# HGRN values projected token-major in the front and loaded by the heads, four gates turned into fillers

## The chip, the cores and the metric

The kernel runs on one NeuronCore of a Trainium2 chip. The metric is the time of one execution on the device in microseconds (us), the median of several runs. The engines named are PE (TensorE matmul; PEld its weight load), DVE (VectorE), ACT (ScalarE), POOL (GpSimd) and SP (SyncE, which issues most DMAs).

## The reference, cut to what matters

One layer of a hybrid mixer: 512 latent tokens `x` and 256 context tokens `ctx`, model width 1024. Both are normalised and modulated, and multiplied by one wide matrix `w_in`. Its columns feed branch A (four heads of gated DeltaNet), branch B (four heads of HGRN2) and 24 groups of 128 gate columns, which only the latent tokens need. For branch B each head has 128 columns for q, for the values `i_b` and for the two forget gates:

```python
(qkv, a_f, a_b, be_f, be_b, g_a, q_b, i_b, f_f, f_b, g_b, m_a, m_b) = split_last(h @ w_in, IN_SIZES)
q_b = to_heads(jax.nn.silu(q_b), H_B).astype(f32)
v_b = to_heads(i_b, H_B).astype(f32)
...
# HGRN2, per chunk: S_t = diag(f_t) S_{t-1} + k_t v_t^T with k_t = 1 - f_t
s_next = f_end_c[..., None] * s + jnp.einsum('bhck,bhcv->bhkv', k_end_c, v_c)
att = jnp.einsum('bhik,bhjk,bhijk->bhij', q_c, k_c, pair)
o = jnp.einsum('bhck,bhkv->bhcv', q_c * jnp.exp(lg_c), s) + jnp.einsum('bhij,bhjv->bhiv', att, v_c)
...
return (jax.nn.sigmoid(m_a) * ya + jax.nn.sigmoid(m_b) * yb) @ w_out
```

The context is scanned in both directions for the state alone, then the latent tokens. The values of all 768 tokens are used; the outputs of the mixers are normalised, gated, projected up, merged, multiplied by `w_out` and added to `x`; a SwiGLU with its own modulation follows.

## The kernel before, in words

Every large product is done in float32 precision as three matmuls of reduced-precision parts (high x high, high x low, low x high). `split` loads a piece of weight to `raw`, ACT casts it to `hi` (L100), DVE subtracts for `lo` (L102), and `mm3` issues the three matmuls for each of the eight slices of 128 model columns (L110). The normalised tokens stand as `hhi`, `hlo` (latent, 512) and `chi`, `clo` (context, 256), with the model dimension on the partitions.

The front normalises the latent tokens slice by slice and feeds each slice at once to six accumulating products `pg0`, which are gates 16 to 21; their weights come as `wr` (128x768, one DMA for each slice, L239). Gates 22 and 23 (`rest[0:2]`) follow with code whose priority is lowered by 1500, with four quarters of the second modulation (`mwe`, `pmo`). A finished gate is copied by ACT to `gt` (L136) and stored to `gdram` (L137), from where it is loaded only after the mixers. `pab` is a small projection for branch A's decay.

The mixers are Python generators: `gdn_pair(0)` and `gdn_pair(2)` are streams G0 and G2 (two DeltaNet heads each), `hgrn(h)` is H0 to H3. The string `PLAN` says in which order steps of the streams are written: "H0:2" runs H0 for two yields, "F:2" writes two gates as fillers (`gate_low`), "N" and "aT" are modulation quarters. Behind X the branch A buffers are gone; the gates that are left and the rest of the modulation (`mwb`, issued on POOL's queue) are written with a priority lower by 5000, so they fill whatever H2's last steps leave open. A scheduler places each engine's instructions by priority and readiness, so an instruction may stand far from where its code is; each engine then executes in order.

An HGRN head has three projections (`h_z0`, `h_z1` for the forget gates over all tokens, `h_z2` for q), eight attention levels (`att`: level 7 and then `LEVELS` 0 to 6, four matmuls `h_pA` each, DVE operations `kq` L556, `AT` L536, `K` L558, `L` L559), then `values()`, then the two scans (`h_pk`, `h_pS`), the output `h_po` and its norm (`h__pt`, `h_y`). `values()` splits the head's 128 value columns, projects 512 latent and 256 context tokens with features on partitions (`h_zv`), copies them to `Z`, and transposes six blocks (`h_pv`) into `vh`, tokens on partitions. A DeltaNet pair builds `p_N`, inverts triangular blocks by 30 small DVE steps (`p_o1` to `p_o30` on `p_Z`), transposes the result (`p_T1`, `p_T2`, L745 and L746), scans, and ends with the transposes `p_pt` for its two heads.

After the mixers `branch` loads gates (`ug`) and mixer outputs (`uy`) from memory, `up` is the up-projection (`pup`), then `w_out` (`pwo`) and the SwiGLU (`pf`, `pfo`).

Of the kernel before, what the change touches and what calls it, by code (L numbers as in the profile page):

```python
# [7 lines left out]
F32 = mybir.dt.float32  # L8
# [5 lines left out]
P = 128  # L14
D = 1024
KT = 8
CTX = 256
SEQ = 512
TOK = 768
NH = 4  # L20
# [3 lines left out]
C_QKV, C_AB, C_GA, C_QB, C_IB, C_FF, C_FB, C_GB, C_MA, C_MB = (  # L24
    0, 1536, 1552, 2064, 2576, 3088, 3600, 4112, 4624, 5648)
# [3 lines left out]
MK = 4  # L29

PLAN = ("H0:1 G0:6 F:1 H1:3 G0:4 F:1 G2:3 G0:5 F:2 N:1 G0:1 H0:2 "
        "F:1 G0:99 H0:99 F:3 G2:4 H1:99 G2:4 F:1 G2:99 N:1 H3:99 aT:1 H2:1 X H2:99")


def shape_constants():
# [13 lines left out]
def body(tc, T, out, tap=None):  # L49
    nc = tc.nc  # L50
    PSUM = bass.MemoryType.PSUM
    W_IN = T["w_in"][0]
# [5 lines left out]
    with ExitStack() as root:  # L58
        def pool(name, bufs=1, side=None, **kw):
            return tc.tile_pool(name=name, bufs=bufs, side=side, reuse_waits="tile", **kw)  # L60
# [7 lines left out]
        dr = root.enter_context(tc.tile_pool(name="dr", bufs=1, space=bass.MemoryType.DRAM))  # L68
# [7 lines left out]
        def bank(tag, name):  # L76
            return ps_.tile([P, 512], F32, name=name, tag=tag, bufs=BANKS[tag])

        def pmm(name):
            return bank("mm", name)  # L80
# [3 lines left out]
        def split(srcs, kt, n, pool=None, dst=None):  # L84

            WN[0] += 1
            pool = pool or ring["w"]
            raw = pool.tile([P, kt, n], F32, name=f"raw{WN[0]}", tag="raw", bufs=2)
            c0 = 0
            for s in srcs:  # L90
                w = s.shape[1]
                nc.sync.dma_start(raw[:, :, c0:c0 + w], s.rearrange("(k p) f -> p k f", p=P))
                c0 += w
            if dst is not None:
                hi, lo = dst
                nc.scalar.copy(hi, raw[:, :, :])
                nc.vector.tensor_tensor(lo, raw[:, :, :], hi.bitcast(F32), op=ALU.subtract)
                return hi, lo
            hi = pool.tile([P, kt, n], F32R, name=f"hi{WN[0]}", tag="hi")
            nc.scalar.copy(hi[:, :, :], raw[:, :, :])  # L100
            lo = pool.tile([P, kt, n], F32R, name=f"lo{WN[0]}", tag="lo")
            nc.vector.tensor_tensor(lo[:, :, :], raw[:, :, :], hi.bitcast(F32), op=ALU.subtract)  # L102
            return hi, lo

        def mm3(ps, a, b, kt, start=True, stop=True):

            n, tot = 0, 3 * kt
            for k in range(kt):
                for u, v in ((0, 0), (0, 1), (1, 0)):
                    nc.tensor.matmul(ps, a[u](k), b[v](k), start=(start and n == 0), stop=(stop and n == tot - 1))  # L110
                    n += 1
# [6 lines left out]
        def feat(w, src, n, name, t0=0, tag="mm"):  # L118

            ps = bank(tag, name)  # L120
            mm3(ps[:, 0:n], [lambda k, t=t: t[:, k, :] for t in w], [lambda k, t=t: t[:, k, t0:t0 + n] for t in src], KT)
            return ps
# [5 lines left out]
        lat, ctx = (hhi, hlo), (chi, clo)  # L128
        gdram = dr.tile([24, P, SEQ], F32, name="gdram")
        ydram = dr.tile([8, P, SEQ], F32, name="ydram")  # L130
        gcols = [C_GA + P * i for i in range(4)] + [C_GB + P * i for i in range(4)]
        gcols += [C_MA + P * i for i in range(8)] + [C_MB + P * i for i in range(8)]

        def gate_out(i, ps, pool, tag="raw"):
            gt = pool.tile([P, SEQ], F32, name=f"gt{i}", tag=tag, bufs=3 if pool is ring.get("sp") else 2)
            nc.scalar.copy(gt[:, :], ps[:, :])  # L136
            nc.sync.dma_start(gdram[i, :, :], gt[:, :])  # L137
# [36 lines left out]


        NG0 = 6
        rest = [22, 23] + list(range(16))
        gs = early.enter_context(pool("gs"))
        s3_stack = ExitStack()
        s3 = s3_stack.enter_context(pool("s3"))  # L180
        with ExitStack() as st:
            s1 = st.enter_context(pool("s1"))
            sp = ring["sp"] = st.enter_context(pool("sp", 2))
# [15 lines left out]
            ident, UI, LI, US, LS = (sq[:, k * P:(k + 1) * P] for k in range(5))  # L199
# [35 lines left out]
            for d0, d1 in groups:  # L235
                load_mod(d0, d1)
                for e in range(d0, d1):
                    wr = wrs.pop() if wrs else s1.tile([P, NG0 * P], F32, name=f"wr{e}", tag="wr", bufs=5)
                    nc.sync.dma_start(wr[:, :], W_IN[P * e:P * e + P, C_MB:C_MB + NG0 * P])  # L239
                    wraws.append(wr)  # L240
                if d0 == 1:
                    r0 = 0
                    for key, pat_, cnt in small[1]:
                        kw = {"k": P} if key == "lb_logits" else {"p": P}
                        nc.sync.dma_start(rows[1][r0:r0 + cnt, :], T[key].rearrange(pat_, **kw) if pat_ else T[key])
                        r0 += cnt
# [95 lines left out]
            pg0 = [bank(t, f"pg0_{i}") for i, t in enumerate(("mm", "mm", "ga", "ga", "ga", "fa"))]  # L342
# [13 lines left out]
            for d in range(KT):  # L356
                if d in nxt:
                    modulation(*groups[nxt[d]])
                if d + 1 < KT:
                    prepare(d + 1)  # L360
                if d == 6:
                    norm_rows((0, 1))
                wh, wl = wparts[d]
                for n, (u, v) in enumerate(((wh, hhi), (wl, hhi), (wh, hlo))):
                    for i in range(NG0):
                        nc.tensor.matmul(pg0[i][:, :], u[:, P * i:P * i + P], v[:, d, :],
                                         start=(d == 0 and n == 0), stop=(d == KT - 1 and n == 2))
            for i in range(NG0):
                gate_out(16 + i, pg0[i], sp, "gt")
            for d in range(KT):  # L370
                normed(d, 1, (0, 1), chi, clo, "ha")
            dump("chi", chi.bitcast(F32))
# [26 lines left out]
            for i in rest[0:2]:  # L399
                w = [s1.tile([P, KT, P], F32R, name=f"rw{i}{j}") for j in range(2)]  # L400
                w = split([W_IN[:, gcols[i]:gcols[i] + P]], KT, P, dst=[t[:, :, :] for t in w])
                gate_out(i, feat(w, lat, SEQ, f"pgate{i}"), sp, "gt")
            for q in quarters[0:4]:
                mod_now(*q, s1.tile([P, KT, 256], F32, name="mwe%d%d" % q, tag="mw", bufs=6), nc.sync)
            del quarters[0:4]
# [3 lines left out]
        with s3_stack:  # L409
# [4 lines left out]
            for src, o, n in ((ctx, 0, CTX), (lat, CTX, SEQ)):  # L414
                ps = pmm(f"pab{o}")
# [23 lines left out]
            e = s3.tile([P, 6, 8], F32, name="e")  # L439
            nc.vector.scalar_tensor_tensor(e[:, :, :], zz[:, :, :], -1.0, zz[:, :, :], op0=ALU.mult, op1=ALU.max)  # L440
            nc.scalar.activation(e[:, :, :], e[:, :, :], AF.Exp, scale=-1.0)
            t = s3.tile([P, 6, 8], F32, name="t")
# [41 lines left out]
        def hgrn(h):  # L484

            n = f"h{h}_"
# [3 lines left out]
            q = hg.tile([P, SEQ], F32, name=n + "q", tag="q", bufs=2)  # L490
            vh = hg.tile([P, 6, P], F32, name=n + "v", tag="v")

            def values():
                w = split([W_IN[:, C_IB + P * h:C_IB + P * h + P]], KT, P)
                Z = hg.tile([P, TOK], F32, name=f"{n}Zv", tag="Z", bufs=2)
                for src, a, t in ((lat, CTX, SEQ), (ctx, 0, CTX)):
                    ps = feat(w, src, t, f"{n}zv_{a}")
                    nc.scalar.copy(Z[:, a:a + t], ps[:, 0:t])
                for g, cnt in ((0, 4), (4, 2)):
                    pv = pmm(f"{n}pv{g}")  # L500
                    for i in range(cnt):
                        nc.tensor.transpose(pv[:, P * i:P * i + P], Z[:, P * (g + i):P * (g + i + 1)], ident)
                    nc.scalar.copy(vh[:, g:g + cnt, :], pv[:, 0:P * cnt].rearrange("p (g k) -> p g k", k=P))

            for d in range(3):
                w = split([W_IN[:, (C_FB, C_FF, C_QB)[d] + P * h:(C_FB, C_FF, C_QB)[d] + P * h + P]], KT, P)
                m = TOK if d < 2 else SEQ
                Z = hg.tile([P, TOK], F32, name=f"{n}Z{d}", tag="Z", bufs=2)
                sg = hg.tile([P, TOK], F32, name=f"{n}sg{d}", tag="sg")
                for src, a, t in ((lat, 0, SEQ), (ctx, SEQ, CTX))[0:1 + (d < 2)]:  # L510
                    ps = feat(w, src, t, f"{n}z{d}_{a}")
                    nc.scalar.copy(Z[:, a:a + t], ps[:, 0:t])

                nc.scalar.activation(sg[:, 0:m], Z[:, 0:m], AF.Abs)
                nc.scalar.activation(sg[:, 0:m], sg[:, 0:m], AF.Exp, scale=-1.0)
# [42 lines left out]
                nc.vector.tensor_tensor(Kv, Kv, view(L[:, 1, :], 2 * b - 1, [(1 - 2 * b - TOK, 2), n2b, (0, b)]), op=ALU.subtract)  # L558
                nc.vector.tensor_tensor(Lv, Lv, view(L[:, 0, :], b, [(TOK - 1, 2), n2b, (0, b)]), op=ALU.add)  # L559
            yield  # L560
            values()
            QG = hg.tile([P, 2, SEQ], F32, name=n + "QG", tag="kq", bufs=2)
            nc.scalar.activation(QG[:, :, :], L[:, :, 0:SEQ], AF.Exp)
            ed = hg.tile([P, 2, 4], F32, name=n + "ed", tag="ed")
# [349 lines left out]
        hg = early.enter_context(pool("hg"))  # L914
# [9 lines left out]
                if done:  # L924
                    break

        gates = rest[2:]

        def filler(n):
            for _ in range(n):  # L930
# [4 lines left out]
        for item in before.split():  # L935
            name, n = item.split(":")
# [26 lines left out]
        for item in after.split():  # L963
            name, n = item.split(":")
# [6 lines left out]
        with pool("yp", 1) as yp, pool("mg", 1) as mg:  # L971
# [52 lines left out]
            with pool("xp", 2) as xp:  # L1024
# [44 lines left out]
                for kk in range(4):  # L1069
                    w = weights(0, kk)  # L1070
# [18 lines left out]
        with pool("ff", 2) as ff:  # L1089
# [43 lines left out]
            for half in range(2):  # L1133
# [7 lines left out]
                for kk in range(NKK - 2):  # L1141
                    w = split([W[256 * kk:256 * kk + 256, cs]], 2, 512)
# [3 lines left out]
                for g in range(4):  # L1146
                    for w, kk in zip(ws, (NKK - 2, NKK - 1)):
                        part(w, kk, g)
                    t = ff.tile([P, 512], F32, name=f"yt{half}{g}", tag="yt")
# [37 lines left out]
```

## Time and profile before

| what | value |
|---|---|
| median of 3 runs | 1082.74 us (1082.46 to 1085.16) |
| profiled execution, its own time | 1084.9 us |
| its span, first to last instruction | 1083.2 us |
| mean granted TensorE clock | 0.983 |
| PE busy | 1018.9 us, 94% |
| DVE busy | 659.3 us, 61% |
| ACT busy | 549.2 us, 51% |
| first branch A matmul `g_k_zl` | 102.4 us |
| last transposes `p_pt` of G2 | 518.9 us |
| first up-projection matmul `pup` | 602.2 us |

Busy shares are means over stages with different limits; the stretches of the profile by stage tell which engine is full where. A PE matmul's listed duration reaches into the next one, so the cost of one in a row is the distance between two starts.

### The profile page before, as it was taken

To read this page: it belongs to the slowest core of one execution; us is meant where nothing else is said; L and a number is where in the kernel's file an instruction comes from. 1 tells how busy PE (TensorE), PEld (TensorE's weight loads), DVE (VectorE), ACT (ScalarE), POOL (GpSimd) and SP (SyncE) were. 2 spreads that over 40 slices of the span, in tenths; PEclk is the share of its full clock that TensorE was granted. 3 is DMA by queue.
4 is the path that set the end of the run, shared out by engine and by line. 5 is a ranking of instruction groups with operands and counts; after the bars stand their busy time and mean duration, and the time that the engine had idled before them with its cause. 6 is when DMAs were issued, how large, how long until landed. Compare 5 with 4: busy or idle time off the path is not lost.

```text
span 1083.2 us, 16716 instructions
## 1 busy us (share of the span) xinstructions
PE 1018.9 (94%) x6567; PEld 843.8 (78%) x6567; DVE 659.3 (61%) x1246; ACT 549.2 (51%) x1037; POOL 72.4 (7%) x129
## 2 busy tenths in 40 slices
PE   4999999889999999899989899999999999999996
PEld 2587888777897887798767688798888878888785
DVE  3375686789767968875795565777343433422524
ACT  4373678658867765876764643442222222221212
POOL 1000000400001021001101000011000000000000
PEclk9999999989999999999899999999999999999998
DMA  9953222112004123102636643546333323322222
GB/s 315 344 182 114 60 57 61 50 58 69 3 25 142 50 68 88 51 2 96 203 120 220 226 157 119 154 138 192 96 98 94 97 84 98 97 97 97 89 97 87
DMA packets 139649, 121.72 MB, mean 112 GB/s; under 512 B 5533, under 2 KB 116531, under 8 KB 139571
## 3 DMA queue, kind: packets, MB, share of 16 engines
q1 hardware_dynamic: 133923, 104.05, 31.0%
q0 software_dynamic: 3552, 13.11, 3.6%
q10 hardware_dynamic: 2096, 3.50, 1.0%
q8 instruction: 51, 0.84, 0.3%
q14 instruction: 27, 0.22, 0.1%
HBM read 110.16 MB, written 10.49 MB: 111 GB/s over the span
## 4 chain that ended last, share of the span: by engine, by line
PE 43%; DVE 4%; DMA 4%; issue 3%; ACT 3%; POOL 1%; SPq 0%; POOLq 0%; ACTq 0%; DVEq 0%
PE pf L110 22%; PE pfo L110 10%; PE pup L110 3%; DMA uy<-ydram 1%; PE pgate L110 1%; PE pwo L110 1%; PE h_pA L531 1%; DMA mwb<-in_mod_w_dram 1%; DVE lo L102 1%; ACT hi L100 1%; PE p_s_pk L835 1%; PE p_s_pk L844 1%; DVE acc L878 0%; DMA ug<-gdram 0%; PE h_z L110 0%
## 5 line engine op out<-in xcount | busy, mean ns | idle before, releaser
L100 ACT CAST hi<-raw 128x1024 fp32r<-128x1024 f32 (+1 forms) x129 | 127.6, 991 | 274.2 <-PE pf L110 96.6
L102 DVE TENSOR_TENSOR lo<-raw,hi 128x1024 fp32r<-128x1024 f32 (+1 forms) x129 | 148.0, 1147 | 171.0 <-ACT hi L100 170.6
L110 PE MATMUL pf<-hhi,hi 128*128 128x512 f32 (+1 forms) x352 | 133.8, 381 | 0.0
L110 PE MATMUL pf<-hhi,lo 128*128 128x512 f32 (+1 forms) x352 | 133.7, 380 | 0.0
L110 PE MATMUL pf<-hlo,hi 128*128 128x512 f32 (+1 forms) x352 | 133.7, 380 | 0.0
L110 PEld LDWEIGHTS pf<-hlo,hi 128*128 128x128 f32 x352 | 66.2, 188 | 12.7 <-DVE hlo L1067 0.2
L110 PEld LDWEIGHTS pf<-hhi,lo 128*128 128x128 f32 x352 | 66.2, 188 | 12.7 <-DVE lo L102 0.2
L110 PEld LDWEIGHTS pf<-hhi,hi 128*128 128x128 f32 x352 | 66.1, 188 | 12.3
L110 PE MATMUL pfo<-lo,uh 128*128 128x512 f32 x176 | 68.8, 391 | 0.1
L110 PE MATMUL pfo<-hi,ul 128*128 128x512 f32 x176 | 68.5, 389 | 0.0
L110 PE MATMUL pfo<-hi,uh 128*128 128x512 f32 x176 | 67.9, 390 | 0.0
L110 PE MATMUL pgate<-hhi,hi 128*128 128x512 f32 x128 | 52.9, 413 | 4.1 <-ACT hi L100 4.0
L110 PE MATMUL pgate<-hhi,lo 128*128 128x512 f32 x128 | 52.4, 410 | 4.3 <-DVE lo L102 4.3
L110 PE MATMUL pgate<-hlo,hi 128*128 128x512 f32 x128 | 51.9, 405 | 0.0
L1123 DVE TENSOR_TENSOR sg<-sg,pf 128x512 f32<-128x512 f32 x22 | 15.1, 687 | 49.4 <-PE pf L110 49.4
L878 DVE SCALAR_TENSOR_TENSOR acc<-mwb,sc,acc 128x256 f32<-128x256 f32 x72 | 34.4, 480 | 9.9 <-DMA mwb<-in_mod_w_dram 8.6
L110 PE MATMUL h_z<-hhi,hi 128*128 128x512 f32 x96 | 39.7, 413 | 0.0
L110 PEld LDWEIGHTS pfo<-lo,uh 128*128 128x128 f32 x176 | 33.0, 188 | 7.8 <-DVE lo L102 1.0
L110 PE MATMUL h_z<-hlo,hi 128*128 128x512 f32 x96 | 39.0, 406 | 0.0
L110 PE MATMUL h_z<-hhi,lo 128*128 128x512 f32 x96 | 38.5, 401 | 0.0
L110 PEld LDWEIGHTS pfo<-hi,uh 128*128 128x128 f32 x176 | 32.8, 188 | 7.3 <-ACT hi L100 0.7
L110 PEld LDWEIGHTS pfo<-hi,ul 128*128 128x128 f32 x176 | 33.0, 188 | 6.8
(449 smaller groups left out, 2518.4 us busy)
## 6 DMA issues: line engine op xcount, KB each, us to landing
raw<-in_ffn_w_in_dram SPq DMA_DIRECT2D x44, 512.0 KB, 3.8
raw<-in_w_in_dram SPq DMA_DIRECT2D x37, 512.0 KB, 3.7
raw<-in_ffn_w_out_dram SPq DMA_DIRECT2D x22, 512.0 KB, 3.5
mwb<-in_mod_w_dram POOLq DMA_DIRECT2D x18, 512.0 KB, 4.7
mw<-in_mod_w_dram SPq DMA_DIRECT2D x16, 512.0 KB, 6.0
gdram<-gt SPq DMA_DIRECT2D x24, 256.0 KB, 2.2
raw<-in_w_in_dram SPq DMA_DIRECT2D x18, 256.0 KB, 2.9
mwe<-in_mod_w_dram SPq DMA_DIRECT2D x4, 1024.0 KB, 7.7
```

What stands on the lines that cost most here:

```text
L100: nc.scalar.copy(hi[:, :, :], raw[:, :, :])
L102: nc.vector.tensor_tensor(lo[:, :, :], raw[:, :, :], hi.bitcast(F32), op=ALU.subtract)
L110: nc.tensor.matmul(ps, a[u](k), b[v](k), start=(start and n == 0), stop=(stop and n == tot - 1))
L531: nc.tensor.matmul(pA[:, P * c:P * c + P], kq[:, 0, P * c:P * c + P], kq[:, 1, P * c:P * c + P], start=True, stop=True)
L835: nc.tensor.matmul(pk[:, P:2 * P], N[:, d, e, g, :], rt[:, :], start=True, stop=True)
L844: nc.tensor.matmul(pk[:, 2 * P:3 * P], kend[:, :], u[:, :], start=True, stop=True)
L878: nc.vector.scalar_tensor_tensor(acc[:, :], mw[:, k - k0, :], sc[:, k:k + 1], acc[:, :], op0=ALU.mult, op1=ALU.add)
L1123: nc.vector.tensor_tensor(sg[:, :], sg[:, :], pgu[1][:, :], op=ALU.mult)
```

## The change

The four HGRN heads' value columns are contiguous in `w_in`, 512 in all. The front's six products become four latent value products, in which `hhi` or `hlo` (128 tokens) is the stationary operand and 512 weight columns move, and gates 16 and 17. Their weights come as two DMAs for each slice (256 KB and 128 KB) in place of one of 384 KB. `value_out` copies a finished group of 128 tokens x 512 columns and stores it to `vdram`. Gates 18 and 19 are the two of lowered priority; behind them come the context tokens' values, two products `pv0` and `pv1` over four weight pieces of 2 x 512 columns. `values()` is gone; a head loads its six blocks with one DMA (384 KB in runs of 512 B) issued by SP. The plan has 20 gates for fillers where it had 16, and three more of them ahead of X (twelve for nine).

```diff
 PLAN = ("H0:1 G0:6 F:1 H1:3 G0:4 F:1 G2:3 G0:5 F:2 N:1 G0:1 H0:2 "
-        "F:1 G0:99 H0:99 F:3 G2:4 H1:99 G2:4 F:1 G2:99 N:1 H3:99 aT:1 H2:1 X H2:99")
+        "F:2 G0:99 H0:99 F:3 G2:4 H1:99 F:1 G2:4 F:2 G2:99 N:1 H3:99 aT:1 H2:1 X H2:99")
...
+        vdram = dr.tile([6, P, NH * P], F32, name="vdram")
...
-        rest = [22, 23] + list(range(16))
+        rest = [18, 19, 20, 21, 22, 23] + list(range(16))
...
-                    nc.sync.dma_start(wr[:, :], W_IN[P * e:P * e + P, C_MB:C_MB + NG0 * P])
+                    nc.sync.dma_start(wr[:, 0:4 * P], W_IN[P * e:P * e + P, C_IB:C_IB + 4 * P])
+                    nc.sync.dma_start(wr[:, 4 * P:], W_IN[P * e:P * e + P, C_MB:C_MB + 2 * P])
...
-                    for i in range(NG0):
-                        nc.tensor.matmul(pg0[i][:, :], u[:, P * i:P * i + P], v[:, d, :],
-                                         start=(d == 0 and n == 0), stop=(d == KT - 1 and n == 2))
-            for i in range(NG0):
-                gate_out(16 + i, pg0[i], sp, "gt")
+                    ends = dict(start=(d == 0 and n == 0), stop=(d == KT - 1 and n == 2))
+                    for i in range(4):
+                        nc.tensor.matmul(pg0[i][:, :], v[:, d, P * i:P * i + P], u[:, 0:4 * P], **ends)
+                    for i in range(4, NG0):
+                        nc.tensor.matmul(pg0[i][:, :], u[:, P * i:P * i + P], v[:, d, :], **ends)
+
+            def value_out(g, ps):
+
+                vt = sp.tile([P, NH * P], F32, name=f"vt{g}", tag="gt", bufs=3)
+                nc.scalar.copy(vt[:, :], ps[:, :])
+                nc.sync.dma_start(vdram[g, :, :], vt[:, :])
+
+            for i in range(4):
+                value_out(2 + i, pg0[i])
+            for i in range(4, NG0):
+                gate_out(12 + i, pg0[i], sp, "gt")
...
+            del rest[0:2]
+            pv = [pmm(f"pv{g}") for g in range(2)]
+            for kk in range(4):
+                w = split([W_IN[2 * P * kk:2 * P * kk + 2 * P, C_IB:C_IB + 4 * P]], 2, 4 * P)
+                for g in range(2):
+                    mm3(pv[g][:, :], [lambda k, t=t: t[:, 2 * kk + k, P * g:P * g + P] for t in ctx],
+                        [lambda k, t=t: t[:, k, :] for t in w], 2, start=(kk == 0), stop=(kk == 3))
+            for g in range(2):
+                value_out(g, pv[g])
...
-            def values():
-                w = split([W_IN[:, C_IB + P * h:C_IB + P * h + P]], KT, P)
-                Z = hg.tile([P, TOK], F32, name=f"{n}Zv", tag="Z", bufs=2)
...
-            values()
+            nc.sync.dma_start(vh[:, :, :], vdram[:, :, P * h:P * h + P].rearrange("g p v -> p g v"))
...
-        gates = rest[2:]
+        gates = rest
```

Three places show what the change moves. In the rows, a name's trailing number is the tile's own; `hi`, `lo` and `rw` are weight parts, `lev` a mask.

PE at the end of the front, before: the second gate of lowered priority and then branch A's small projection.

```order
L331 MATMUL px17_675<-sq_91,xt1_116 128x128
L110 MATMUL pgate23_741<-hlo_74,rw230_735 128x512
L110 MATMUL pgate23_741<-hhi_73,rw231_736 128x512
L110 MATMUL pgate23_741<-hhi_73,rw230_735 128x512
L110 MATMUL pgate23_741<-hlo_74,rw230_735 128x512
L110 MATMUL pgate23_741<-hhi_73,rw231_736 128x512
L110 MATMUL pgate23_741<-hhi_73,rw230_735 128x512
L110 MATMUL pgate23_741<-hlo_74,rw230_735 128x512
L110 MATMUL pgate23_741<-hhi_73,rw231_736 128x512
L418 MATMUL pab0_859<-chi_75,wab2_855 32x256
```

After, at the end of gate 19:

```order
L110 MATMUL pgate19_750<-hhi_73,rw190_744 128x512
L110 MATMUL pgate19_750<-hlo_74,rw190_744 128x512
L110 MATMUL pgate19_750<-hhi_73,rw191_745 128x512
L110 MATMUL pv0_778<-hi3_782,chi_75 128x512
L110 MATMUL pv0_778<-lo3_784,chi_75 128x512
L110 MATMUL pv0_778<-hi3_782,clo_76 128x512
L110 MATMUL pv0_778<-hi3_782,chi_75 128x512
L110 MATMUL pv0_778<-lo3_784,chi_75 128x512
L110 MATMUL pv0_778<-hi3_782,clo_76 128x512
L110 MATMUL pv1_779<-hi3_782,chi_75 128x512
L110 MATMUL pv1_779<-lo3_784,chi_75 128x512
L110 MATMUL pv1_779<-hi3_782,clo_76 128x512
```

The context values' 48 matmuls stand between the gate and `pab0`, ahead of the first head's projection.

DVE around the transpose that ends G2's inversion, before:

```order
L737 TENSOR_TENSOR p2_o29_4379<-p2_Z_4252 128x58
L739 TENSOR_TENSOR p2_Z_4252<-p2_Z_4252,p2_o29_4379 128x2x29
L524 TENSOR_TENSOR h3_q_4980<-h3_Z2_5122,h3_sg2_5123 128x512
L737 TENSOR_TENSOR p2_o30_4382<-p2_Z_4252 128x30
L556 TENSOR_TENSOR h3_kq0_5169<-h3_q_4980,h3_E0_5170 128x512
L739 TENSOR_TENSOR p2_Z_4252<-p2_Z_4252,p2_o30_4382 128x30
L102 TENSOR_TENSOR lo53_5833<-raw53_5829,hi53_5831 128x1024
L745 STREAM_TRANSPOSE p2_T1_4386<-p2_Z_4252 128x32x32
L746 STREAM_TRANSPOSE p2_T2_4387<-p2_Z_4252 128x32x32
L536 COPY_PREDICATED h3_AT_5156<-lev_685,h3_pA0_5174 128x512
L556 TENSOR_TENSOR h3_kq1_5182<-h3_q_4980,h3_E1_5183 128x512
```

And after:

```order
L747 TENSOR_TENSOR p2_o29_4452<-p2_Z_4285 128x58
L569 TENSOR_TENSOR h3_L_5052<-h3_L_5052 128x2x16x16
L749 TENSOR_TENSOR p2_Z_4285<-p2_Z_4285,p2_o29_4452 128x2x29
L546 COPY_PREDICATED h3_AT_5229<-lev_694,h3_pA4_5299 128x512
L747 TENSOR_TENSOR p2_o30_4455<-p2_Z_4285 128x30
L566 TENSOR_TENSOR h3_kq5_5307<-h3_q_5053,h3_E5_5308 128x512
L749 TENSOR_TENSOR p2_Z_4285<-p2_Z_4285,p2_o30_4455 128x30
L568 TENSOR_TENSOR h3_K_5051<-h3_K_5051,h3_L_5052 128x2x8x32
L755 STREAM_TRANSPOSE p2_T1_4459<-p2_Z_4285 128x32x32
L756 STREAM_TRANSPOSE p2_T2_4460<-p2_Z_4285 128x32x32
L102 TENSOR_TENSOR lo47_4387<-raw47_4383,hi47_4385 128x512
L546 COPY_PREDICATED h3_AT_5229<-lev_694,h3_pA5_5312 128x512
```

Before, head 3 has begun its level 0 when `p2_T1` comes; now its levels 1 to 5 stand ahead of it.

PE in head 2, before: the end of its value projection, a gate and the transposes of the values.

```order
L110 MATMUL h2_zv_0_6073<-clo_76,hi55_6042 128x256
L110 MATMUL h2_zv_0_6073<-chi_75,lo55_6044 128x256
L110 MATMUL pgate9_5527<-hhi_73,hi46_5523 128x512
L110 MATMUL pgate9_5527<-hlo_74,hi46_5523 128x512
L110 MATMUL pgate9_5527<-hhi_73,lo46_5525 128x512
L502 MATMUL h2_pv0_6099<-sq_91,h2_Zv_6046 128x128 x4
L502 MATMUL h2_pv4_6105<-sq_91,h2_Zv_6046 128x128 x2
L110 MATMUL pgate9_5527<-hhi_73,hi46_5523 128x512
L110 MATMUL pgate9_5527<-hlo_74,hi46_5523 128x512
```

And after, between G2's last `p2_1_pt` and head 2's first level product:

```order
L110 MATMUL h2_z2_0_5943<-hhi_73,lo62_5939 128x512
L116 MATMUL pmo32_5431<-ones_101,mwe32_5420 32x1 x8
L110 MATMUL pgate8_5532<-hhi_73,hi53_5528 128x512
L110 MATMUL pgate8_5532<-hlo_74,hi53_5528 128x512
L110 MATMUL pgate9_5608<-hhi_73,hi54_5604 128x512
L110 MATMUL pgate9_5608<-hlo_74,hi54_5604 128x512
L110 MATMUL pgate8_5532<-hhi_73,lo53_5530 128x512
L110 MATMUL pgate8_5532<-hhi_73,hi53_5528 128x512
L110 MATMUL pgate8_5532<-hlo_74,hi53_5528 128x512
L110 MATMUL pgate8_5532<-hhi_73,lo53_5530 128x512
L110 MATMUL pgate8_5532<-hhi_73,hi53_5528 128x512
L541 MATMUL h2_pA7_5982<-h2_kqd_5976 128x128 x4
```

The value projection is gone from there: nine matmuls of `h2_z2` (the last opens these rows) and nine of gates 8 and 9 are left between the two.

More of the change, by code (lines that the diff above doesn't have):

```diff
@@ L491, in hgrn @@
             vh = hg.tile([P, 6, P], F32, name=n + "v", tag="v")
-            def values():
-                w = split([W_IN[:, C_IB + P * h:C_IB + P * h + P]], KT, P)
-                Z = hg.tile([P, TOK], F32, name=f"{n}Zv", tag="Z", bufs=2)
[L496 to L503, printed above, removed]
             for d in range(3):
```

## The prediction

> **What bounds the kernel now.** First the page's busy shares, then stretches cut at the program's stages (columns: stretch, length, PE, PEld, DVE, ACT, POOL busy with counts, granted TensorE clock, DMA share, GB/s).
>
> ```profile
> span 1083.2 us, 16716 instructions
> PE 1018.9 (94%) x6567; PEld 843.8 (78%) x6567; DVE 659.3 (61%) x1246; ACT 549.2 (51%) x1037; POOL 72.4 (7%) x129
> ...
> 0.00:70.00 70.00, 53.58 (x388) 35.30 (x389) 29.36 (x73) 30.22 (x45) 4.38 (x11) 0.98 0.88 277
> 70.00:102.00 32.00, 31.18 (x228) 23.79 (x227) 22.37 (x80) 13.84 (x30) 0.46 (x10) 1.00 0.58 185
> 102.00:205.00 103.00, 101.89 (x729) 86.24 (x726) 73.38 (x117) 76.63 (x133) 10.22 (x24) 1.00 0.22 61
> 205.00:261.00 56.00, 49.68 (x322) 40.79 (x320) 51.15 (x115) 35.82 (x58) 8.67 (x20) 0.91 0.24 67
> ...
> 404.00:445.00 41.00, 38.78 (x209) 32.94 (x208) 37.47 (x85) 26.20 (x42) 6.08 (x9) 1.00 0.27 77
> 445.00:519.00 74.00, 67.63 (x758) 59.08 (x756) 49.53 (x118) 53.75 (x156) 7.30 (x6) 0.98 0.17 55
> 519.00:602.00 83.00, 76.75 (x429) 64.05 (x428) 64.66 (x117) 52.45 (x89) 8.58 (x11) 0.95 0.59 187
> 602.00:656.00 54.00, 49.04 (x289) 39.81 (x288) 34.15 (x53) 27.91 (x40) 0.00 (x0) 0.97 0.56 183
> 656.00:1083.00 427.00, 413.97 (x1986) 343.05 (x1984) 190.97 (x270) 126.36 (x179) 11.32 (x17) 0.99 0.34 108
> ```
>
> PE is the bound nearly everywhere: 94% of the span, 97% from 656 on, which the change leaves alone. The exceptions matter: the front waits for DMA (share 0.88), 205 to 261 and 404 to 445 are DVE's (51.15 of 56, 37.47 of 41). So I count PE work first, and then ask whether the places where PE waits get longer. The profiled execution took 1084.9 us for a span of 1083.2; the median run, 1082.74, lies 2.2 below it. My sum is a difference, put on the median.
>
> **The change part by part.** Prices of the value projection, from PE's timeline (start, length, tile), the tile rows (min/median/max ns) and the DMA issues:
>
> ```profile
> 252.69 0.28 PE L110 MATMUL h_zv<-chi,hi 128*128 128x256 f32 x1
> ...
> 255.44 0.28 PE L110 MATMUL h_zv<-chi,lo 128*128 128x256 f32 x1
> ...
> 257.80 0.82 PE L502 MATMUL h_pv<-sq,h_Zv 128*128 128x128 f32 x6
> 525.83 0.39 PE L110 MATMUL h_z<-hhi,lo 128*128 128x512 f32 x1
> ...
> 530.59 0.39 PE L110 MATMUL h_z<-hhi,lo 128*128 128x512 f32 x1
> L498 ACT COPY h_Zv<-h_zv x8: 356/470/587, 253.0 to 539.3; 128x512 f32<-128x512 f32 x4, 128x256 f32<-128x256 f32 x4
> L503 ACT COPY h_v<-h_pv x8: 373/514/647, 258.7 to 541.5; 128x512 f32<-128x512 f32 x4, 128x256 f32<-128x256 f32 x4
> L136 ACT COPY gt<-pgate x18: 562/582/607, 79.6 to 605.2; 128x512 f32<-128x512 f32 x18
> L100 ACT CAST hi<-raw x129: 602/1053/1149, 71.6 to 1062.5; 128x1024 fp32r<-128x1024 f32 x111, 128x512 fp32r<-128x512 f32 x18
> L102 DVE TENSOR_TENSOR lo<-raw,hi x129: 671/1224/1228, 73.2 to 1063.6; 128x1024 fp32r<-128x1024 f32 x111, 128x512 fp32r<-128x512 f32 x18
> L239 SPq DMA_DIRECT2D wr<-in_w_in_dram x8: 360/1322/3221, 6.7 to 36.5; - x8
> wr<-in_w_in_dram SPq DMA_DIRECT2D x8, 384.0 KB, 8.6
> gdram<-gt SPq DMA_DIRECT2D x24, 256.0 KB, 2.2
> raw<-in_w_in_dram SPq DMA_DIRECT2D x37, 512.0 KB, 3.7
> ```
>
> Back to back, a matmul costs the distance of starts: 2.75 us over 23 steps, 0.120 us, at 256 columns; 4.76 over 21, 0.227, at 512; the transposes (0.82 - 0.28)/5 = 0.11.
>
> PE: the 96 latent value matmuls of 512 columns and four gates' 96 change places. Context values cost 4 x 24 x 0.120 = 11.5 before and 48 x 0.227 = 10.9 now; 24 transposes (2.6) go. Total 10.9 - 11.5 - 2.6 = -3.2 us.
>
> ACT: 16 copies go (8 x 0.47 + 8 x 0.51 = 7.9), six value copies (6 x 0.58 = 3.5) come. Splits: each head's `values()` had one of 128x1024, and the four of the token-major context weights replace these; the four gates that came through `wr` now need one each: +4 x 1.05 = 4.2 on ACT, +4 x 1.22 = 4.9 on DVE. ACT's balance is 4.2 + 3.5 - 7.9, nothing; DVE's +4.9 lies under PE's work except around p2_T1 (below). POOL's modulation loads keep their places in the plan.
>
> Front: PE gets 10.9 more after the gates, so the mixers start some 11 us later (11 to 12.5: the projection's splits queue on DVE). DVE has room there (22.37 of 32).
>
> The `wr` load becomes two DMAs, 16 issues for 8. Floor: nothing, since several are in flight and the queue is waiting for DMA engines (8.6 us to land, against 3.7 for a larger raw). Ceiling: 8 x 1.32 = 10.6 us of SP's queue in series. I take 0.5: the bytes are the same.
> The Trainium skill, "DMA: Bandwidth & Descriptors", section "Anatomy of one DMA — SWDGE (gpsimd) path", gives each DMA on that path a fixed 2.0 us besides its bytes; eight more in series would by it be 16 us, an estimate, and the sum 1094 to 1095; these DMAs are issued by SP, and no run here shows the fixed part alone.
>
> Head loads: 384 KB from memory instead of a split. They are issued on SP behind the previous head's stored output, because `vh` has one buffer and the load waits for that head's last read of it; behind it wait that head's y store and filler weights. A raw takes 3.7 us to land, and a head's levels and scan take 34.4 us (below), so I cost the loads at nothing; without that cover they are 4 us each, at most 16.
>
> Until G2's chain ends, PE's work changes so. The context values add 10.9. Four latent value groups and 12 gate fillers, against pg0's four further gates and nine fillers, add three projections of 24 x 0.227 = 5.44: +16.3. Heads 0, 1 and 3 lose 2.87 + 5.44 + 0.65 each: -26.9. Part of head 2's h2_z1 and h2_z2 comes ahead of that end (15 + 3 matmuls of 512, 24 of 256): +7.0. Sum +7.3. Behind it: head 2's values -9.0, the pulled part -7.0, one more gate +5.44: -10.5. Together -3.2 again.
>
> How G2 ends and what follows, in three rows of DVE's timeline, pieces of the chain of waits (start, length, what) and one row of PE's waits between 602 and 656 (total, times, longest):
>
> ```profile
> 444.48 2.04 DVE L745 STREAM_TRANSPOSE p_T<-p_Z 128x1024 f32<-128x1024 f32 x1
> ...
> 448.81 0.67 DVE L556 TENSOR_TENSOR h_kq<-h_q,h_E 128x512 f32<-128x512 f32 x1
> 449.40 0.69 DVE L558 TENSOR_TENSOR h_K<-h_K,h_L 128x512 f32<-128x512 f32 x1
> ...
> 513.76 2.68 POOL p_hs L475
> ...
> 519.10 0.21 PE p_pt L480
> ...
> 519.97 4.64 DMA mwb<-in_mod_w_dram
> 524.65 7.35 issue
> ...
> 545.90 2.05 PE h_pA L531 x16
> ...
> 580.25 0.33 PE h__pt L480
> ...
> 602.49 3.33 DMA uy<-ydram
> ...
> PE pup L110 <- DVE x L1001: 4.7, 2, 3.8
> ```
>
> p2_T1 (the transpose at 444.48) now stands on DVE behind 19 operations of head 3's levels 1 to 5, 0.6 to 0.7 us each (11 to 13 us), and six more splits (some 5): about 18 us. It would start between +11 (DVE's queue fits into what PE's lateness allows) and +24 (nothing of it does); I take +18. The scan from there to the last p_pt (74.5 us, PE 67.63 of 74) loses the heads' level work already done: PE's count falls 2.6, DVE's 10, so 66 to 70 us. G2's end, 519, then moves by +7.3 (PE's waits unchanged) to +20 (the transpose at +24, the scan only 4 shorter); I take +18 less the middle of the scan's 4.5 to 8.5, 11.5, and drawn a little towards the PE count to +10.5.
>
> From G2's end to the first up-projection: 602.2 - 519.0 = 83.2 us now, with 70.0 of PE work counted by the prices above, of which 59.5 remains. Head 2's first level product stands 27 us behind G2's end (545.90), after z1, z2 and values; now only 9 matmuls of z2 and pgate8's first nine precede it, and its wait is pgate8's weights, whose buffer comes free with G2's end, and q's ACT and DVE steps. Between 7 and 17 us; I take 11. The levels to h__pt stay 34.4 us (580.25 - 545.90), and the gates behind them 21.9 plus four: 71.3, which is 11.9 less.
>
> Up-projection: the ug, uy and mg loads hold PE (5 us idle in 602 to 656, 4.7 of it in PE's waits there, last row); head 2's y is stored some 5 us earlier against this point, worth 0 to 5, I take 2.6. Sum: +10.5 - 11.9 - 2.6 = -4.0: **1078.7 us**. Counting PE's work alone gives -3.2.
>
> **The rivals.**
> 1. Slower. G2 pays DVE's queue in full: p2_T1 at +24, the scan only 4 shorter, G2's end at +20, then -11.9 and 0 to -2: +6 to +8, 1089. For it speaks DVE's 37.47 of 41 just ahead; against it that fewer levels remain in the scan. It decides from a G2 end of about +15.
> 2. No change: G2's end at +12, and the up-projection's loads still late: 1082.6.
> 3. More than counted: the added fillers fill PE's waits in G2's scan (74 - 67.6 = 6.4) and the loads at the up-projection (4) are hidden: -3.2 - 6.4 - 1 to 4, some 1071. Against it: those waits stood there with fillers at hand before.
> 4. `wr` in series: +10.6 in the front on top of -4, 1089. The DMA share of 0.88 over 70 us speaks for a front that feels it, the nearly equal bytes against.
> 5. At G2's end PE idles and the clock drops. The two rows show it now:
>
> ```profile
> 497.00:519.00 22.00, 18.48 (x112) 15.35 (x112) 11.32 (x35) 12.70 (x41) 5.54 (x4) 0.94 0.42 144
> 519.00:532.00 13.00, 13.00 (x91) 11.09 (x90) 9.93 (x22) 9.34 (x13) 1.56 (x2) 0.83 0.75 223
> ```
>
> A clock of 0.83 over 13 us costs 2.2 us. With z1 and z2 used up, PE could stay idle for the 11 us to the first level and run its next 6 us slowly, +3 more: 1082, again no change.
> The Trainium skill, "TensorE: Matmul & The Clock Gate", Part 1 on the clock gate, says that the array's clock halves after a window of about 3.4 us without activity and returns after a busy one; the trace's drop behind G2's wait agrees.
>
> **How the numbers follow.** Forecast 0.42 (own range 1074 to 1081), rival 1 0.23, rivals 2 and 5 0.18, rival 3 0.13, rival 4 0.04. The range reaches to rivals 1 and 3: 1068 to 1091. Within 0.3% (1079.5 to 1086.0) is about what a measurement of this kernel cannot tell from no change. Faster: 0.42 x 0.85 + 0.13 = 0.49; same 0.42 x 0.15 + 0.18 = 0.24; slower 0.27.
>
> **What would show it.** g0_k's first matmul 11 us later; h_pv gone; p2_T1 near 462; the last p_pt near 529; the first pup near 601; 427 us from pup's end on unchanged. Wrong if the head loads make h_pS or h_po wait for a DMA, if p2_T1 comes after 468, or if the front grows by more than 13.

## The result: slower, and the profile after

The changed kernel took 1101.66 us (median of 4 runs, 1098.89 to 1103.07) against 1083.95 for the kernel before beside it: ratio 1.0154, 95% interval 1.0136 to 1.0173. The forecast was 1078.7, range 1068 to 1091. Across experiments ratios to the kernel before are compared, since its median was 1083.95 to 1086.21 in the different sets.

The page's first rows, after:

```profile
span 1101.3 us, 16647 instructions
...
PE 1023.2 (93%) x6495; PEld 840.3 (76%) x6495; DVE 660.7 (60%) x1253; ACT 551.0 (50%) x1034; POOL 72.2 (7%) x129
```

PE has 72 instructions fewer and 3.2 us less work by the prices of the prediction, yet is busy 4.3 us longer (1023.2 for 1018.9), and its time without work grew from 64.3 to 78.1 us. The loss is waiting, and a slower clock behind the waits.

To see where, both executions are cut at the same events: first `g_k_zl`; then, from the first step of G2's inversion, `p_T1`, the last `p_pt`, head 2's first `h_pA`, the last `h__pt`, the first `pup`, the last `pup` (columns as in the prediction). Before:

```profile
0.00:102.40 102.40, 84.95 (x616) 59.21 (x616) 52.13 (x152) 44.46 (x75) 4.84 (x21) 0.98 0.78 247
407.10:444.50 37.40, 35.18 (x190) 29.91 (x189) 34.46 (x80) 23.53 (x35) 3.13 (x5) 1.00 0.27 78
444.50:519.30 74.80, 68.43 (x766) 59.64 (x768) 50.03 (x119) 54.24 (x156) 7.30 (x6) 0.98 0.16 54
519.30:545.90 26.60, 25.47 (x159) 21.73 (x159) 22.56 (x42) 20.45 (x30) 3.81 (x5) 0.92 0.71 213
545.90:581.40 35.50, 30.38 (x178) 25.26 (x179) 31.85 (x61) 19.42 (x41) 4.77 (x6) 0.95 0.44 143
581.40:602.20 20.80, 20.80 (x94) 17.17 (x93) 10.41 (x15) 12.79 (x20) 0.00 (x0) 1.00 0.68 231
602.20:656.40 54.20, 49.24 (x290) 40.00 (x289) 34.02 (x52) 28.03 (x41) 0.00 (x0) 0.97 0.56 184
```

After:

```profile
0.00:116.30 116.30, 97.23 (x663) 69.11 (x663) 58.80 (x156) 50.96 (x84) 4.73 (x21) 1.00 0.75 236
424.30:468.80 44.50, 41.39 (x225) 33.88 (x224) 41.98 (x98) 25.62 (x40) 2.12 (x3) 1.00 0.22 66
468.80:538.80 70.00, 64.25 (x716) 55.38 (x715) 40.49 (x103) 52.81 (x152) 5.83 (x6) 0.95 0.19 63
538.80:555.10 16.30, 7.20 (x50) 4.55 (x49) 14.30 (x30) 13.17 (x19) 1.55 (x2) 0.71 0.76 229
555.10:590.60 35.50, 32.55 (x196) 27.33 (x195) 30.37 (x58) 19.47 (x41) 4.77 (x6) 0.99 0.45 139
590.60:624.50 33.90, 28.88 (x112) 22.53 (x110) 19.23 (x34) 17.50 (x26) 2.29 (x3) 0.90 0.75 242
624.50:674.00 49.50, 47.67 (x290) 38.77 (x289) 31.38 (x49) 23.90 (x35) 0.00 (x0) 1.00 0.55 181
674.00:1101.00 427.00, 413.89 (x1985) 342.93 (x1983) 190.82 (x269) 125.79 (x179) 11.33 (x17) 0.99 0.34 108
```

The front ends 13.9 us later. The inversion takes 7.1 longer, the scan behind it 4.8 less, and G2 ends 19.5 late. Behind it the first stretch shrinks by 10.3, but PE idles in 9.1 of its 16.3 us (length less PE busy) and gets a clock of 0.71. Head 2's levels take 35.5 in both. The gates left over then need 33.9 us instead of 20.8, five of them idle, at a clock of 0.90. The up-projection gives 4.7 back, and the last 427 us are the same.

What PE waited for in those two stretches, on PE, ACT and SP (in brackets the idle time before, and what ended it):

```profile
550.42 0.79 PE L110 MATMUL pgate<-hhi,hi 128*128 128x512 f32 x1 [6.53 <-ACT hi L100]
...
553.40 0.63 PE L110 MATMUL pgate<-hhi,hi 128*128 128x512 f32 x1
553.83 0.63 PE L110 MATMUL pgate<-hlo,hi 128*128 128x512 f32 x1
...
602.37 0.50 PE L110 MATMUL pgate<-hhi,lo 128*128 128x512 f32 x1 [2.46 <-DVE lo L102]
```

```profile
549.32 1.04 ACT L100 CAST hi<-raw 128x1024 fp32r<-128x1024 f32 x1 [1.24 <-DMA raw<-in_w_in_dram]
550.27 0.63 ACT L526 ACTIVATE h_sg<-h_sg 128x512 f32<-128x512 f32 x1
...
553.40 0.62 ACT L554 COPY h_kqd<-h_q 128x512 f32<-128x512 f32 x1 [1.03 <-DVE h_q L534]
```

```profile
539.69 0.32 SPq L504 DMA_DIRECT2D ydram<-p_oa  x1
540.11 1.14 SPq L92 DMA_DIRECT2D raw<-in_w_in_dram  x2
```

And from the chain of waits:

```profile
540.01 7.85 DMA mwb<-in_mod_w_dram
...
593.22 7.38 DMA mwb<-in_mod_w_dram
...
601.10 1.22 DVE lo L102
```

All eight gates written behind X take their weight buffers from what G2 gives up, so the first load is issued at 540.11, behind G2's last store on SP, beside two mwb loads, and the cast can start at 549.32. Until then PE has nine matmuls of h_z2. Head 2's first level could not have started before 554.0 even with PE free: its operand `kqd` is copied from q by ACT at 553.40, and q's own steps (`h_sg` at 550.27) stand behind that cast in ACT's order. Later `lo` stands on DVE behind sums that wait for an mwb load of 7.4 us.

### The profile page after: what moved, and what is told of

It reads as the page before. It is cut to its first block, busy times and chain, and to the rows that moved or that the text cites. A ratio compares the mean times of both kernels' runs of the same rounds, so it can differ in the third digit from the quotient of the medians.

```text
span 1101.3 us, 16647 instructions
## 1 busy us (share of the span) xinstructions
PE 1023.2 (93%) x6495; PEld 840.3 (76%) x6495; DVE 660.7 (60%) x1253; ACT 551.0 (50%) x1034; POOL 72.2 (7%) x129
## 4 chain that ended last, share of the span: by engine, by line
PE 63%; DVE 10%; DMA 9%; issue 8%; ACT 6%; POOL 2%; SPq 1%; POOLq 0%; DVEq 0%; ACTq 0%
PE pf L110 18%; PE pfo L110 10%; PE h_z L110 6%; PE pgate L110 4%; DMA mwb<-in_mod_w_dram 4%; PE pup L110 3%; DVE lo L102 2%; DMA wr<-in_w_in_dram 2%; PE pg L369 2%; PE g_q_zl L110 1%; PE h_pA L541 1%; PE g_k_zl L110 1%; ACT hi L100 1%; DMA mwe<-in_mod_w_dram 1%; PE p_s_pk L845 1%
## 5 line engine op out<-in xcount | busy, mean ns | idle before, releaser
L100 ACT CAST hi<-raw 128x1024 fp32r<-128x1024 f32 (+1 forms) x136 | 132.3, 974 | 285.0 <-PE pf L110 93.4
L102 DVE TENSOR_TENSOR lo<-raw,hi 128x1024 fp32r<-128x1024 f32 (+1 forms) x136 | 153.4, 1129 | 175.3 <-ACT hi L100 174.4
L110 PE MATMUL pgate<-hhi,hi 128*128 128x512 f32 x160 | 69.7, 436 | 15.5 <-ACT hi L100 15.5
L110 PE MATMUL pgate<-hhi,lo 128*128 128x512 f32 x160 | 68.8, 431 | 8.4 <-DVE lo L102 8.3
L110 PE MATMUL pgate<-hlo,hi 128*128 128x512 f32 x160 | 67.7, 423 | 0.0
L110 PEld LDWEIGHTS pgate<-hhi,hi 128*128 128x128 f32 x160 | 32.2, 201 | 25.5 <-ACT hi L100 20.8
L110 PEld LDWEIGHTS pgate<-hhi,lo 128*128 128x128 f32 x160 | 32.0, 200 | 18.4 <-DVE lo L102 13.0
```

## The experiments

**The two-piece weight load of the front** (the kernel before otherwise):

```diff
-nc.sync.dma_start(wr[:, :], W_IN[P * e:P * e + P, C_MB:C_MB + NG0 * P])
+nc.sync.dma_start(wr[:, 0:4 * P], W_IN[P * e:P * e + P, C_MB:C_MB + 4 * P])
+nc.sync.dma_start(wr[:, 4 * P:], W_IN[P * e:P * e + P, C_MB + 4 * P:C_MB + 6 * P])
```

> The kernel before, with only the gate weights of the front loaded by two DMAs a slice (256 KB and 128 KB) in place of one. Theory A (the front's 14 us of lateness are the context values' 11 plus waits on DVE; the load in two pieces is hidden): 1083 to 1085, the first g_k_zl at 102 to 104. Theory B (the second DMA of each slice stands on SP's queue and delays the front): 1088 or more, g_k_zl at 106 or later.

1086.09 against 1085.86, ratio 1.000 (0.998 to 1.002); g_k_zl at 102.5. Rival 4 is out.

**No context values.**

```diff
-            pv = [pmm(f"pv{g}") for g in range(2)]
...
+                nc.vector.memset(vt[:, :], 1.0)
```

> The changed kernel without the context values' splits and matmuls: ones are stored in their place, so the states from the context are wrong; everything else stands in the same order. It prices the context values in the front. Theory A (lateness of the front goes through to the end one to one): g_k_zl at 104 to 106, total 1088 to 1091 (11 to 14 less than the changed kernel). Theory B (DVE or the loads behind G2 set the end, and the front's lateness is absorbed): 1096 to 1101.

1087.13, ratio 1.0014 (0.9993 to 1.0034), g_k_zl at 102.2, both a little below theory A's ranges. The front's lateness is the context values' and goes through to the end: 1.4% of the time (good to 0.3%), some 15 us for 10.9 us of matmuls and their splits. The stretches behind are those of the changed kernel, shifted:

```profile
409.10:453.60 44.50, 41.40 (x225) 33.87 (x224) 41.98 (x98) 25.73 (x40) 2.11 (x3) 1.00 0.23 66
...
523.60:540.00 16.40, 7.15 (x50) 4.55 (x49) 14.32 (x30) 13.26 (x19) 1.55 (x2) 0.71 0.75 224
```

**Context values back in the heads.** Latent values stay in the front; a head splits its columns again, projects the context and transposes two blocks:

```diff
-nc.sync.dma_start(vh[:, :, :], vdram[:, :, P * h:P * h + P].rearrange("g p v -> p g v"))
+nc.sync.dma_start(vh[:, 2:6, :], vdram[2:6, :, P * h:P * h + P].rearrange("g p v -> p g v"))
+w = split([W_IN[:, C_IB + P * h:C_IB + P * h + P]], KT, P)
+ps = feat(w, ctx, CTX, f"{n}zv")
...
```

> The changed kernel, but the context tokens' values go back to the heads (24 matmuls of 256 columns, two transposes), the latent ones stay in the front; the order of DVE between the first step of G2's inversion and p2_T1 has 11 operations of heads again, as before the change, where the changed kernel has 28. Theory A (lateness from the front plus heads' operations between the inversion's steps): g_k_zl at 103 to 105, the inversion (first p_o to p_T) 36 to 38 us in place of 44, total 1080 to 1088. Theory B (the loss is made by the four gates that became fillers and by what stands behind G2's end): 1094 or more.

1094.62, ratio 1.0077 (1.0054 to 1.0099); outside theory A's 1080 to 1088 and just inside B's. The inversion took 38.4 us with 11 operations of heads, near A's 36 to 38, and G2 ended at 518.8 (519.3 before the change). But PE got two gates fewer done by then (gate 7 to 15 behind it, 9 to 15 before), and from there to the last pup it took 143.6 us, against 137.1 before the change. So a G2 that ends on time isn't enough.

**The plan of before**, eleven gates behind X instead of eight:

```diff
-"F:2 G0:99 H0:99 F:3 G2:4 H1:99 F:1 G2:4 F:2 G2:99 N:1 H3:99 aT:1 H2:1 X H2:99"
+"F:1 G0:99 H0:99 F:3 G2:4 H1:99 G2:4 F:1 G2:99 N:1 H3:99 aT:1 H2:1 X H2:99"
```

> The changed kernel with the plan of before: nine gates written ahead of X, eleven behind. DVE has 37 operations of heads among the inversion's steps of G2 (28 with the changed plan, 11 before). Theory A (each such operation lengthens the inversion by some 0.45 us, and gates behind X have no cover at G2's end): inversion 47 to 49 us, total 1104 to 1112. Theory B (the plan's new fillers crowd G2 and make it late): 1090 to 1098.

1118.78, ratio 1.0301 (1.0263 to 1.0340): beyond theory A's 1104 to 1112, with an inversion of 49.7 us where A said 47 to 49. The new plan is worth 16 us of a change that would cost 33 with the old one.

```profile
418.90:468.60 49.70, 37.09 (x196) 30.78 (x195) 45.85 (x104) 27.66 (x41) 1.87 (x3) 0.89 0.15 48
```

DVE has little idle time in the inversion in all of these (41.98 us busy of 44.5 in the changed kernel, 45.85 of 49.7 here). Its 61 step operations are listed with 21.6 to 21.9 us in all; 11, 28 and 37 operations of heads with 8.6, 19.8 and 25.6, and the inversion takes 37.4, 44.5 and 49.7. So an operation of a head is listed with 0.7 us, but each one more lengthens the inversion by 0.4 to 0.5 us (7.1 for 17, 12.3 for 26), as theory A had it, because listed durations on DVE overlap. In the changed kernel, a step alone and one with a head's operation behind it:

```profile
432.23 0.33 DVE L749 TENSOR_TENSOR p_Z<-p_Z,p_o 128x168 f32<-128x168 f32 x1
432.59 0.35 DVE L747 TENSOR_TENSOR p_o<-p_Z 128x184 f32<-128x184 f32 x1
...
457.97 0.32 DVE L749 TENSOR_TENSOR p_Z<-p_Z,p_o 128x168 f32<-128x168 f32 x1
458.22 0.68 DVE L566 TENSOR_TENSOR h_kq<-h_q,h_E 128x512 f32<-128x512 f32 x1
458.82 0.30 DVE L747 TENSOR_TENSOR p_o<-p_Z 128x150 f32<-128x150 f32 x1
```

From one step's start to the next it is 0.36 us alone and 0.85 with the operation between.

**Head 3's products on POOL.**

```diff
-nc.vector.tensor_tensor(kq[:, 1, :], q[:, :], E[:, :], op=ALU.mult)
+(nc.gpsimd if h == 3 else nc.vector).tensor_tensor(kq[:, 1, :], q[:, :], E[:, :], op=ALU.mult)
```

> The changed kernel with head 3's seven q times E products on POOL instead of DVE: 24 operations of heads among the inversion's steps of G2 instead of 28. Theory A (each lengthens the inversion by some 0.45 us): 42 us in place of 44, total 1098 to 1101. Theory B (the steps wait for each other, DVE's other work fits between): inversion still 44, total 1100 to 1104, with POOL's longer operation holding the levels.

1104.66, ratio 1.0199 (1.0168 to 1.0229). Four operations fewer, but an inversion of 47.2 us: both theories miss. DVE's timeline and then POOL's show why:

```profile
446.70 0.38 DVE L747 TENSOR_TENSOR p_o<-p_Z 128x220 f32<-128x220 f32 x1
447.11 1.35 DVE L749 TENSOR_TENSOR p_Z<-p_Z,p_o 128x220 f32<-128x220 f32 x1
448.49 0.38 DVE L747 TENSOR_TENSOR p_o<-p_Z 128x210 f32<-128x210 f32 x1
```

```profile
446.86 1.35 POOL L566 TENSOR_TENSOR h_kq<-h_q,h_E 128x512 f32<-128x512 f32 x1 [22.64 <-DVE h_q L534]
```

The DVE step that starts at 447.11, behind the start of POOL's operation, takes 1.35 us where its neighbours take 0.38. All step operations together take 24.6 us in place of 21.6, which eats the relief.

**Four gates left out.** Gates 20 to 23 are stored as copies of gate 17, `rest` begins with 18, 19, 0.

```diff
+            for i in range(20, 24):
+                gate_out(i, pg0[5], sp, "gt")
```

> The changed kernel without the four gates that lost their place in the front: gates 20 to 23 are stored as copies of gate 17, so four of the eight gates behind G2's end are gone (PE work -21.8 us). Theory A (behind G2 PE first has nothing ready and then has the gates left over, which set when the up-projection starts): last p_pt to first pup falls from 85.7 to 64 to 70 us, total 1082 to 1087. Theory B (the ten mwb loads and DVE's sums over them pace that stretch): it stays at 78 us or more, total 1094 or more.

1087.51, ratio 1.0023 (1.0001 to 1.0045). The stretch from the last p_pt to the first pup falls from 85.7 to 65.4 us, 20.3 of the four gates' 21.8; the up-projection then takes 54.2 again, so its gain of 4.7 is lost. At this place a gate is not a filler: it is on the path.

**The late modulation behind all gates** (its steps were six for each gate):

```diff
                 gate(gates.pop(0), ring["mod"], wx, "ga")
-            mod_steps(6)
+            else:
+                mod_steps(6)
```

> The changed kernel with the steps of the late modulation (mwb loads and their sums on DVE) written behind all gates instead of six for each gate. Theory A (gates are late since nothing is ready at G2's end): last p_pt to first pup 82 to 86 us, total 1098 to 1103. Theory B (the gates' weight parts stand on DVE behind sums that wait for mwb): that stretch at 76 us or less, total 1090 to 1096, unless the loads then hold the product with w_out.

1099.01, ratio 1.0127 (1.0095 to 1.0159), its interval overlapping the changed kernel's. The stretch falls to 77.7 us, by 8, between the theories; the up-projection takes 54.3 instead of 49.5. So the sums do hold gates, but most of what is gained there is lost again behind it.

**Two gates written behind H3 instead of ahead of G2's scan** ("H3:99 F:2 aT:1").

> The changed kernel with two of the fillers written behind H3 instead of before G2's scan, so that a gate whose weights are already in place stands on PE between the last p_pt and head 2's first level product. Theory A (PE's 9 us without work behind G2, and the slow clock after it, are a loss that a ready gate fills): idle there under 3 us, total 1092 to 1097. Theory B (the gate only delays head 2's levels, and the fillers are missed in the scan): 1099 to 1104.

1105.78, ratio 1.0196 (1.0176 to 1.0216): theory B, a little beyond it. Idle at G2's end falls to 4.1 us, but PE idles 7.7 and 9.5 us in inversion and scan, and two gates more stand at the end.

**Two of the eight gates behind X with weights in a free buffer**, nothing taken from before:

```diff
-        while gates or mods:
-            if gates:
+        while len(gates) > 2 or mods:
+            if len(gates) > 2:
...
-"aT:1 H2:1 X H2:99"
+"aT:1 H2:1 X F:2 H2:99"
```

> The changed kernel with two of the eight gates behind X made fillers, whose weights come into a buffer that is free before G2's end: a gate's 24 matmuls stand ready between the last p_pt and head 2's first level product, and nothing is taken from before G2's end. Theory A (the 9 us without work there and the slow clock are lost time): idle there under 3 us, last p_pt to first pup 75 to 80 us in place of 85.7, total 1092 to 1098. Theory B (gates are paced by DVE's splits and sums behind G2, so PE waits later instead): 83 us or more, 1099 to 1103.

1095.30, ratio 1.0078 (1.0050 to 1.0105), in theory A's range:

```profile
540.40:555.60 15.20, 11.61 (x70) 8.26 (x70) 13.25 (x27) 13.72 (x20) 1.55 (x2) 0.89 0.67 194
...
609.40:666.80 57.40, 52.01 (x289) 41.47 (x290) 39.19 (x64) 32.86 (x47) 0.00 (x0) 0.91 0.66 203
```

PE idles 3.6 us instead of 9.1 (A said under 3), at a clock of 0.89 instead of 0.71, and it is 69.0 us from the last p_pt to pup instead of 85.7 (A said 75 to 80). The stretch to head 2's first level is only 1.1 us shorter: the gain is work done in it. The up-projection then takes 57.4 instead of 49.5, 5.4 of them idle, for `yh` and `yl`, the parts of the loaded mixer outputs; in the chain of waits `yl` stands behind the late modulation's sums. So half of the gain is kept.

**Both edits.**

> The two edits together: two gates as fillers behind X, and the late modulation written behind all gates. Theory A (two separate losses of the stretch behind G2): last p_pt to first pup 67 to 73 us, of which up to 5 are given back at the up-projection, total 1086 to 1094. Theory B (one loss counted twice): not below 76 us, 1095 to 1100.

1093.07, ratio 1.0067 (1.0041 to 1.0094): 68.6 us to pup and 56.6 of up-projection. The time can't be told from that of the cover alone. What limits both was not tested.

**The values taken out of the kernel before.** Heads load x and ctx as values; no projection, no front work.

```diff
-            values()
+            nc.sync.dma_start(vh[:, 2:6, :], T["x"][0, :, P * h:P * h + P].rearrange("(g p) v -> p g v", p=P))
+            nc.sync.dma_start(vh[:, 0:2, :], T["ctx"][0, :, P * h:P * h + P].rearrange("(g p) v -> p g v", p=P))
```

> The kernel before without the value projections: each head loads 384 KB of raw x and ctx as its values, so the outputs of branch B mean nothing. PE work falls by 4 x 9.0 = 36 us, nothing else is moved; DVE has 33 operations of heads among the inversion's steps of G2 in place of 11. Theory A (values in the mixers mostly filled time in which PE waits anyway; the change's price is then 14 for the context values in the front, 14 for four gates, less what the values were worth, and it came out at +17): worth 8 to 14 us, total 1070 to 1076. Theory B (PE's work is the bound there): worth 30 to 36 us, 1048 to 1054.

1083.44, ratio 0.9978 (0.9957 to 0.9999). 36 us of PE work are worth 2 us, less than either theory said.

```profile
412.90:461.50 48.60, 38.54 (x198) 32.55 (x197) 44.84 (x101) 26.92 (x39) 2.06 (x3) 0.87 0.18 54
...
528.50:545.00 16.50, 6.10 (x44) 3.58 (x43) 14.95 (x32) 11.30 (x16) 1.55 (x2) 0.66 0.68 204
```

Both symptoms of the change are here without the change: an inversion of 48.6 us with heads' operations in it and 10 us of idle PE, and 10.4 us idle behind G2. p2_T1 comes at 461.5, 17.0 us later than before, though the front is not late. Taking the values out of the mixers makes these symptoms.

**The late modulation behind all gates, in the kernel before** (the edit above).

> The kernel before with the late modulation written behind all gates. Theory A (its sums hold DVE under head 2's levels there too, where PE idles 5 us): 1077 to 1082. Theory B (its mwb loads then come beside those of the up-projection, and the time is given back): 1082 to 1088.

1077.11, ratio 0.9908 (0.9885 to 0.9932): theory A, and faster than both kernels. The stretch of head 2's levels (545.9 to 581.4 before, above) now holds 6.4 us more PE work in 2.9 us more time, and the gates behind it need 11.8 us instead of 20.8:

```profile
546.40:584.80 38.40, 36.78 (x217) 30.52 (x218) 35.01 (x66) 21.92 (x44) 4.99 (x6) 1.00 0.51 163
584.80:596.60 11.80, 11.80 (x53) 9.74 (x52) 5.57 (x9) 7.24 (x11) 0.00 (x0) 1.00 0.72 244
```

## Why the prediction was wrong

The sum was G2's end +10.5, the stretch behind it -11.9, the up-projection -2.6. Measured: +19.5, +2.8 and -4.7, which with 0.4 behind it is the span's +18. Of the 22 us between forecast and measurement, 14.7 lie in the stretch behind G2's end and 9.0 in G2's end; the up-projection gave 2.1 more than was taken. Two of the prediction's own signs of being wrong came: p2_T1 at 468.8, after 468, and a front 13.9 us longer, more than 13.

The step that failed is the price of the removed value projections: 9.0 us of PE work for each head was booked as 9.0 us of time, since PE is busy 94%. The kernel without values shows it: 36 us of that work were worth 2. In the prediction's PE count the context values in the front cost +10.9, and what leaves the heads gives -14.1. The runs have some +15 for the first and +1.5 (ratio 1.0014) for the change without it. The projections stood in the heads' streams, ready early, and did two things that the forecast saw but priced too low.

First, they kept head 3 behind. Without them its levels reach DVE during G2's inversion: 28 operations of heads stand there instead of 11, and it takes 44.5 us instead of 37.4. p2_T1 came at +24.3, where +18 was taken and +24 was the bound. But the bound, which the prediction doesn't add up, was not reached by the step named for it, a DVE queue of about 18 us that is paid in full. 13.9 of the 24.3 are the front's, 3.3 come between the front and the inversion, and 7.1 in the inversion; in the kernel without context values, whose front is not late, p2_T1 comes at +9.1. Of the six more splits that were counted none stands in the inversion (7 before, 7 after). So the queue cost 7 there, not 18, and the front's lateness, which was to hide part of the queue, came on top of it in full. The scan behind gave back 4.8, near the "only 4 shorter" of rival 1 (0.23 in the forecast), and G2's end at +19.5 is near its +20. That this rival had the place is in part luck, and its total of 1089 kept the -11.9 behind G2, which did not come.

Second, they covered G2's end. Head 2's z1, z2 and values were 18 us of ready work there. The forecast had z1 and z2 pulled ahead and the values gone, and booked it as 10.5 us less work in the stretch. It was also the work that ran while the first gates' weights were loaded. Rival 5 named this with +3 us. It came as 9.1 us of idle and a clock of 0.71: head 2's first level came 16.3 us after G2's end (11 taken, 7 to 17 the range). The gates behind h__pt took 33.9 us (25.9 taken). Their amount was right, 111 matmuls at 0.227 are 25.2 us, but the wait for late weight parts (5 us idle) and a clock of 0.90 (some 3 us) were not in the sum. Two gates with weights in a free buffer took the kernel from 1.0154 to 1.0078, so this lack of ready work is worth about half of the loss.
The Trainium skill, "TensorE: Matmul & The Clock Gate", Part 1 on the clock gate, has the clock halved behind a window of about 3.4 us without work; the 6.53 us wait ahead of 550.42 and the matmuls 0.43 us apart behind it (553.40, 553.83; 0.227 at full clock) agree. The wait of 2.46 us ahead of 602.37 does not: it is shorter, and yet the matmuls from 603.90 to 606.46 start 0.43 us apart too. So in this kernel shorter waits also cost clock.

The third term is smaller: the front was 13.9 us late (11.1 to 13.5 in seven other kernels with this front), not 11, and none of it was regained, as the kernel without context values shows. Of the 3 us beyond the matmuls, PE's waits between 60 us and the first g_k_zl show 1.4 (2.4 us in place of 1.0, most of it for sums and weight parts on DVE). The rest is open.

Right were: the two-piece load at nothing, the head loads at nothing (no wait on them among PE's waits), head 2's levels unchanged, the up-projection's gain and the last stretch. In ratios (each good to 0.2%, a difference to 0.3%) the change splits like this: values out of the mixers 0.9978, with four more gates as fillers and the new plan 1.0014, with the context values in the front 1.0154. The removal saves 0.2%, its two prices are 0.4% and 1.4%. The split depends on the order, and prices taken singly add up to more than the loss: taken out of the changed kernel, the four gates are worth 1.3% (1.0154 to 1.0023). How much of the loss the inversion alone makes was not isolated: the one run that shortened it, with the context values back in the heads, also gave PE other work.

## What to carry to other kernels

Work of a busy engine is worth its time only where nothing else would end the stretch: before moving it, ask what stood waiting behind it, and price it by a run that leaves it out. Work moved from streams that overlap into a front that has one stream costs all of its time there (here some 15 us for 10.9 of matmuls). When fillers replace early, in-order work, look at where their buffers come free: a filler that becomes ready only at the gap's start doesn't fill it.

## What the runs showed that was not expected

POOL's 128x512 product beside DVE's work stretched a DVE step of 0.38 us to 1.35, about POOL's own 1.35 us, so an idle POOL was no free place for DVE's work. The Trainium skill, "SBUF — State Buffer", section "Who interferes with whom", says that a DVE instruction with two SBUF inputs contends with a GpSimd instruction that reads SBUF, over ports that only one of them can hold at a time; the trace agrees. And six modulation steps for each gate cost the kernel before 0.9%: written behind the gates, the same loads and sums took 1077.11 us.
